# Attention with a bias on one core: scores that stay in PSUM from head to head

## The chip, the cores and the metric

One core of a Trainium2 chip runs the kernel. The metric is the device time of one execution in microseconds (us). Five engines work side by side, each through its own queue in order: TensorE (PE) for matrix products, with its weight loads shown apart (PEld), VectorE (DVE), ScalarE (ACT), GpSimd (POOL), and SyncE (SP), which here only issues transfers (DMAs). Matrix products land in PSUM, a memory of 8 banks, each 128 partitions x 512 float32; everything else lies in SBUF.

## What is computed

```python
batch, n_heads, seq_len, head_dim = 4, 8, 1024, 64          # bias: (1, 1, seq_len, seq_len)
scale = 1.0 / np.sqrt(head_dim)
scores = scale * np.matmul(q, k.transpose(0, 1, 3, 2))
scores = scores + bias
scores_max = np.max(scores, axis=-1, keepdims=True)
attn = np.exp(scores - scores_max) / (np.sum(np.exp(scores - scores_max), axis=-1, keepdims=True) + 1e-8)
return np.matmul(attn, v).astype(np.float32)
```

There are 32 heads of 1024 queries and 1024 keys, all with one bias. Neither kernel subtracts the maximum: the scores are small, and the exps are summed by a column of ones beside v.

## The kernel before

Heads go in 16 pairs (`pr`), queries in halves (`qh`, 512 queries), keys in chunks of 128 (`kc`). A "bank" is one (pair, head, half, chunk): 128 keys x 512 queries of transposed scores, one PSUM bank; there are 512. Three banks share one of two PSUM buffers `ps` (6 of the 8 banks); the last two banks, `xa` and `xb`, serve transposes, the sums `po`, and single banks `pd`.

Per pair, `load_qk` (L75) and `load_v` (L82) issue three kinds of loads on POOL's queue, which cast float32 to bf16 on the way. `transpose_pe` (L86) turns q and k so that the head dimension lies on the partitions: 16 small transposes on PE, then one DVE copy. For q the copy multiplies by `mask`, so that `qT` holds each head beside zeros for the other (L102); `kT` holds both heads of the pair one above the other. `s_fill` (L165) computes three banks with one matmul each, over 128 rows of which the zeros blank out the other head. `s_exp` (L178) is one ScalarE instruction over 128x1536.

The bias enters in two ways. For key chunks of most banks exp(bias) is made once (`b_fill`, `b_exp`, L220 to L233: transposes of `btraw`, then four exps into `eb`), and DVE multiplies each exp by it (`mul_pair`, L235: 1024 or 2048 elements at a time). For the last two chunks of the second half (`late_bias`) PE adds the raw bias, times 1/scale, into PSUM by a second matmul (L176). Six banks, two in each of pairs 3, 7 and 11, have their exp computed on DVE: `d_fill` (L189), `fixed` (L201) and the six steps of `d_steps` (L205), a split into whole and broken powers of two and a polynomial.

`av_bank` (L261) multiplies the exps by v: four pairs of weight load and 65-column matmul a bank, 16 banks to a unit of 512 queries. Its `evac` divides by the ones column on DVE (L279, L281) and SP stores the result. The last pair's second half is done by `av_last` (L296), in two parts.

The order on each engine is written out by a planner (L413 to L764) under `manual_schedule`: it keeps a clock per engine with costs it assumes, and at each turn lets the engine that can start first emit its next piece. The instructions then run in exactly that order, each waiting by semaphores for its inputs. ACT's order is the order of the banks; PE's picks are a fill (`pe_fill`), a transpose (`pe_piece`), a bank for DVE (`pe_d`) or a bank of P times V (`pe_av`).

The lines before that, L327 to L406, start the first pair: part of its k and q comes as float32 on SP's and ACT's queues and is cast on the engines, the first exps are of one and of two banks.

Of the kernel before, what the change touches and what calls it, by code (L numbers as in the profile page):

```python
# [8 lines left out]
F32 = mybir.dt.float32  # L9
# [7 lines left out]
def kernel(  # L17
# [13 lines left out]


    nc = tc.nc
# [6 lines left out]
    HQ = S // 2  # L40
    QC = NCH // 2
# [4 lines left out]
    of = out.rearrange("b h (p c) d -> (b h) p c d", p=P)  # L46
    bf_ = bias.rearrange("a b (p c) k -> p (a b c) k", p=P)

    consts = ctx.enter_context(tc.tile_pool(name="consts", bufs=1))
    raw = ctx.enter_context(tc.tile_pool(name="raw", bufs=3))  # L50
    kvp = ctx.enter_context(tc.tile_pool(name="kvp", bufs=3))
    ep = ctx.enter_context(tc.tile_pool(name="ep", bufs=6))
    op = ctx.enter_context(tc.tile_pool(name="op", bufs=2))
    dp = ctx.enter_context(tc.tile_pool(name="dp", bufs=1))
    de = ctx.enter_context(tc.tile_pool(name="de", bufs=2))
    small = ctx.enter_context(tc.tile_pool(name="small", bufs=4))
    ps_s = ctx.enter_context(tc.tile_pool(name="ps_s", bufs=2, space=bass.MemoryType.PSUM))
    ps_x = ctx.enter_context(tc.tile_pool(name="ps_x", bufs=1, space=bass.MemoryType.PSUM))

    ident = consts.tile([P, P], BF)  # L60
    warm = consts.tile([P, 1], F32)
    btraw = consts.tile([P, NCH, S], BF)
    eb = consts.tile([P, 2, NCH, HQ], BF)
    braw = consts.tile([P, 2, HQ], BF)
    mask = consts.tile([P, 2, HQ], BF)
    vall = consts.tile([P, 2 * NP, NCH, D1], BF)

    k0f = consts.tile([P, 2, QC, D], F32)
    q0f = [consts.tile([P, QC, D], F32, name=f"q0f{t}") for t in range(2)]
    zeros = consts.tile([P, P], BF)  # L70

    raws = {}
    trs = {}

    def load_qk(pr):  # L75
        qr = raw.tile([P, 2, NCH, D], BF, name="qr")
        kr = raw.tile([P, 2, NCH, D], BF, name="kr")
        nc.gpsimd.dma_start(out=kr.rearrange("p t c d -> p t (c d)"), in_=kf[pr])  # L78
        nc.gpsimd.dma_start(out=qr.rearrange("p t c d -> p t (c d)"), in_=qf[pr])  # L79
        raws[pr] = (qr, kr)  # L80
# [5 lines left out]
    def transpose_pe(pr, which, c0, n, tag):  # L86

        src = raws[pr][which]
        px = ps_x.tile([P, n, P], BF, tag=tag, name="px")
        for c in range(n):  # L90
            for t in range(2):
                nc.tensor.transpose(px[t * D:(t + 1) * D, c, :], src[:, t, c0 + c, :], ident[:])  # L92
        if (pr, which) not in trs:
            trs[(pr, which)] = (kvp.tile([P, NCH, P], BF, name="kT") if which else
                                kvp.tile([P, 2, NCH * P], BF, name="qT"))
        dst = trs[(pr, which)]

        def copy():
            if which == 0:

                m = n // QC
                nc.vector.tensor_tensor(  # L102
                    dst[:, :, c0 * P:(c0 + n) * P].rearrange("p t (m q) -> p t m q", m=m),
                    px.rearrange("p (m c) q -> p m (c q)", m=m).unsqueeze(1).to_broadcast([P, 2, m, HQ]),
                    mask.unsqueeze(2).to_broadcast([P, 2, m, HQ]), op=ALU.mult)
            else:
                nc.vector.tensor_copy(dst[:, c0:c0 + n, :], px[:])  # L107
        return copy


    NE = NCH - 2
    DPR = (3, 7, 11)
    banks = [(0, h, 0, kc) for kc in range(NCH) for h in range(2)]

    def mix(early, late, singles):
        while early or late:
            if late and (singles(len(banks), len(early) + len(late)) or not early):
                banks.append(late.pop(0))
            else:
                banks.extend(early[:2])  # L120
                del early[:2]

    for pr in range(NP):
        early = [(pr, h, 1, kc) for kc in range(NE) for h in range(2)]
        late = [(pr, h, 1, kc) for kc in range(NE, NCH - (pr in DPR)) for h in range(2)]
        if pr == NP - 1:
            early = [(pr, h, 1, kc) for h in range(2) for kc in range(NE)]
            late = [(pr, h, 1, kc) for h in range(2) for kc in range(NE, NCH)]
        if pr == 0:
            early += [(1, h, 0, kc) for kc in range(NCH) for h in range(2)]  # L130
            mix(early, late, lambda b, left: b % 3 == 2 and b > 36)
        else:
            if pr > 1:
                banks += [(pr, h, 0, kc) for kc in range(NCH) for h in range(2)]
            mix(early, late, lambda b, left: b % 3 == 2 and (pr < NP - 1 or left > 8))
    NB = len(banks)

    dgroups = []
    for pr in DPR:
        dgroups.append((pr, [len(banks), len(banks) + 1]))  # L140
        banks += [(pr, h, 1, NCH - 1) for h in range(2)]
    assert sorted(banks) == sorted((pr, h, qh, kc) for pr in range(NP) for h in range(2) for qh in range(2) for kc in range(NCH))
    late_bias = {b: x[3] - NE for b, x in enumerate(banks) if x[2] == 1 and x[3] >= NE}
    first_of = {pr: min(b for b in range(NB) if banks[b][0] == pr) for pr in range(NP)}
    d_of = {b: (i, h) for i, (pr, bs) in enumerate(dgroups) for h, b in enumerate(bs)}
    units = {}
    for b in range(len(banks)):
        units.setdefault(banks[b][:3], []).append(b)
    slots = [[0], [1, 2]] + [list(range(i, min(i + 3, NB))) for i in range(3, NB, 3)]
    NS = len(slots)  # L150
    ET = 12
    etiles = {}

    dtiles = {}

    def e_at(b, n):
        if b >= NB:
            return dtiles[d_of[b][0]]["e"][:, d_of[b][1]:d_of[b][1] + n, :]
        if b // ET not in etiles:
            etiles[b // ET] = ep.tile([P, ET, HQ], BF, name="E")  # L160
        return etiles[b // ET][:, b % ET:b % ET + n, :]

    open_ps = {}

    def s_fill(g):  # L165
        if ("S", g) not in open_ps:
            open_ps[("S", g)] = ps_s.tile([P, 3, HQ], F32, tag="s", name="ps")
        ps = open_ps[("S", g)]
        for j, b in enumerate(slots[g]):
            pr, h, qh, kc = banks[b]  # L170
            qT, kT = trs[(pr, 0)], trs[(pr, 1)]
            nc.tensor.matmul(ps[:, j, :], kT[:, kc, :], qT[:, h, qh * HQ:(qh + 1) * HQ],  # L172
                             start=True, stop=b not in late_bias)
        for j, b in enumerate(slots[g]):
            if b in late_bias:
                nc.tensor.matmul(ps[:, j, :], ident[:], braw[:, late_bias[b], :], start=False, stop=True)  # L176

    def s_exp(g):  # L178
        n = len(slots[g])
        nc.scalar.activation(e_at(slots[g][0], n), open_ps.pop(("S", g))[:, :n, :], ACTF.Exp, scale=scale)  # L180

# [5 lines left out]
    LOG2E = 1.4426950408889634  # L187

    def d_fill(b, tag):  # L189
        pr, h, qh, kc = banks[b]  # L190
        ps = ps_x.tile([P, HQ], F32, tag=tag, name="pd")
        nc.tensor.matmul(ps[:], trs[(pr, 1)][:, kc, :], trs[(pr, 0)][:, h, qh * HQ:(qh + 1) * HQ], start=True, stop=False)  # L192
        nc.tensor.matmul(ps[:], ident[:], braw[:, late_bias[b], :], start=False, stop=True)  # L193
        d = d_of[b][0]
        if d not in dtiles:
            dtiles[d] = {"y": dp.tile([P, 2, HQ], I32, name="dy"), "f": dp.tile([P, 2, HQ], F32, name="df"),
                         "p": dp.tile([P, 2, HQ], I16, name="dpw"),
                         "b": dp.tile([P, 2, HQ], F32, name="db"), "e": de.tile([P, 2, HQ], BF, name="de")}

        def fixed():  # L200
            nc.vector.tensor_scalar(dtiles[d]["y"][:, d_of[b][1], :], ps[:], scale * LOG2E * 65536.0, 127.0 * 65536.0,  # L201
                                    op0=ALU.mult, op1=ALU.add)
        return fixed

    def d_steps(d):  # L205
        t = {x: y.rearrange("p h q -> p (h q)") for x, y in dtiles[d].items()}
        t["a"] = t["y"].bitcast(F32)
        lo = t["y"].bitcast(U16).rearrange("p (q w) -> p q w", w=2)[:, :, 0]
        hi = t["y"].bitcast(I16).rearrange("p (q w) -> p q w", w=2)[:, :, 1]
        v = nc.vector  # L210
        return [
            (600, lambda: v.tensor_scalar(t["f"], lo, G / 65536.0, None, op0=ALU.mult)),
            (600, lambda: v.tensor_scalar(t["p"], hi, 0.0, 128.0, op0=ALU.max, op1=ALU.mult)),
            (1140, lambda: v.scalar_tensor_tensor(t["a"], t["f"], U1, t["f"], op0=ALU.add, op1=ALU.mult)),
# [580 lines left out]
```

## Time and profile before

| what | us |
|---|---|
| median of 3 runs (246.30 to 246.69) | 246.63 |
| span of the profiled execution | 246.5 |
| PE idle before fills that waited for an exp (L172, ten times) | 3.3 |
| ACT idle before its first large exp, waiting for PE | 2.6 |
| POOL, loads of v (L84): busy, 32 issues | 28.7 |
| POOL, loads of k and q (L78, L79): busy, 30 issues | 21.2 |
| DVE, products with exp(bias), 2048 elements (L242): busy, 60 | 72.4 |
| DVE, products with exp(bias), 1024 elements (L245): busy, 98 | 64.0 |
| DVE, scaling of results (L281): busy, 63 | 26.7 |
| first exp begins (one bank) / first large exp begins | 5.46 / 9.71 |
| granted PE clock, mean, as a share of full speed | 0.993 |

The profile is of one execution. A row of a group names line, engine, operation, output and inputs, shapes and count; then its busy time in us and the mean duration of one instruction in ns; then the idle time of the engine just before such instructions, and what ended it. Instructions of one engine overlap at their ends, so that the busy time of many is less than count times duration. In the timeline a row has its start, its length, the engine and line, and how many instructions it merges. In the chain of waits the rows have start, length and what the end of the span waited for then.

### The profile page before, as it was taken

Reading aid. Unit: us, or ns where it says so; the run is one execution under the profiler, and the core shown is the slowest. Engines: PE = TensorE matmul, PEld = TensorE weight load, DVE = VectorE, ACT = ScalarE, POOL = GpSimd, SP = SyncE. Lnnn points to the kernel's source line nnn. Section 1 sums busy time; section 2 is a strip of 40 time slices with the busy share of each in tenths; the row PEclk is TensorE's granted clock in tenths of the full one; section 3 lists DMA queues with packets and bytes.
Section 4 is the critical chain, followed back from the end, with each engine's and each line's share of the span. In section 5 each row is a group of like instructions: output and inputs, shape, how many; then the busy total and the mean of one; then the engine's idle time right before and its main releaser. Section 6 shows DMA issues by size and latency. Waiting matters only on the chain.

```text
span 246.5 us, 7234 instructions
## 1 busy us (share of the span) xinstructions
PE 229.9 (93%) x3154; PEld 144.8 (59%) x3207; DVE 219.2 (89%) x366; ACT 236.7 (96%) x181; POOL 55.3 (22%) x76
## 2 busy tenths in 40 slices
PE   8667999999999999999988999999998999999993
PEld 3244656665566656666654665666664566766653
DVE  2417799998999999999999999999999999999994
ACT  5599999999999999999999999999999999999993
POOL 7654333501441304140134000601500000000000
PEclk9799999999999999999999999999999999999999
DMA  5999995995689479492394920792911020202022
GB/s 113 179 197 193 192 131 102 148 84 122 65 123 160 51 122 121 107 116 80 56 127 91 82 88 25 114 122 75 140 45 45 1 88 4 86 1 88 35 77 65
DMA packets 48752, 23.80 MB, mean 97 GB/s; under 512 B 34512, under 2 KB 44624, under 8 KB 48720
## 3 DMA queue, kind: packets, MB, share of 16 engines
q0 software_dynamic: 42560, 14.42, 53.6%
q1 hardware_dynamic: 5872, 8.72, 9.8%
q8 instruction: 25, 0.41, 0.7%
q10 hardware_dynamic: 288, 0.20, 0.3%
q14 instruction: 7, 0.06, 0.1%
HBM read 29.36 MB, written 8.39 MB: 153 GB/s over the span
## 4 chain that ended last, share of the span: by engine, by line
ACT 45%; PE 44%; DVE 4%; DMA 2%; issue 2%; POOL 1%; ACTq 0%; POOLq 0%
ACT E L180 42%; PE ps L172 24%; PE po L269 13%; PE px L92 3%; PE ps L176 3%; ACT eb L232 3%; DMA kr<-in_k_dram 2%; DVE qT L102 1%; DVE E L242 1%; DVE E L239 1%; PE pd L192 1%; PE pd L193 1%; DVE oall L281 1%; DVE db L215 0%; DVE dy L201 0%
## 5 line engine op out<-in xcount | busy, mean ns | idle before, releaser
L180 ACT ACTIVATE E<-ps 128x1536 bf16<-128x1536 f32 (+1 forms) x170 | 227.9, 1525 | 2.8 <-PE ps L172 2.7
L172 PE MATMUL ps<-qT,kT 128*128 128x512 bf16 x454 | 134.9, 382 | 8.2 <-ACT E L180 3.3
L269 PEld LDWEIGHTS <-E 128*128 128x128 bf16 x1992 | 78.9, 98 | 34.1 <-DVE E L242 2.5
L269 PE MATMUL po<-vall,E 128*128 128x65 bf16 x1992 | 84.8, 194 | 0.8 <-DVE E L245 0.3
L242 DVE TENSOR_TENSOR E<-E,eb 128x2048 bf16<-128x2048 bf16 x60 | 72.4, 1217 | 0.0
L245 DVE TENSOR_TENSOR E<-E,eb 128x1024 bf16<-128x1024 bf16 x98 | 64.0, 683 | 4.2 <-ACT eb L232 4.0
L172 PEld LDWEIGHTS <-kT 128*128 128x128 bf16 x506 | 44.9, 97 | 36.6 <-issue 10.2
L84 POOL DMA_DIRECT2D vall<-in_v_dram x32 | 28.7, 902 | 7.1 <-DMA btraw<-in_bias_dram 3.5
L281 DVE TENSOR_TENSOR oall<-po,rs 128x256 f32<-128x256 f32 x63 | 26.7, 425 | 2.2
L78 POOL DMA_DIRECT2D kr<-in_k_dram x15 | 10.5, 699 | 64.5 <-PE px L92 62.4
L102 DVE TENSOR_TENSOR qT<-px,mask 128x2048 bf16<-128x2048 bf16 (+1 forms) x17 | 19.2, 1127 | 5.6 <-PE px L92 5.4
L79 POOL DMA_DIRECT2D qr<-in_q_dram x15 | 10.7, 716 | 48.2 <-PE px L92 47.2
L176 PE MATMUL ps<-braw,ident 128*128 128x512 bf16 x57 | 21.4, 378 | 0.1
L279 DVE RECIPROCAL rs<-po 128x4 f32<-128x4 f32 x63 | 11.2, 178 | 3.3 <-PE po L269 2.5
L107 DVE COPY kT<-px 128x1024 bf16<-128x1024 bf16 (+1 forms) x16 | 10.4, 652 | 0.8 <-PE px L92 0.8
L92 PEld LDWEIGHTS <-qr 128*64 128x64 bf16 x248 | 7.5, 109 | 5.4 <-issue 5.1
L92 PEld LDWEIGHTS <-kr 128*64 128x64 bf16 x240 | 7.2, 109 | 5.0 <-issue 4.7
L92 PE MATMUL px<-ident,qr 128*64 128x128 bf16 x248 | 10.2, 222 | 0.0
L92 PE MATMUL px<-ident,kr 128*64 128x128 bf16 x240 | 9.7, 222 | 0.0
L176 PEld LDWEIGHTS <-ident 128*128 128x128 bf16 x58 | 5.6, 97 | 6.9
L232 ACT ACTIVATE eb<-pb 128x2048 bf16<-128x2048 bf16 (+1 forms) x4 | 6.7, 1676 | 0.0
L226 PEld LDWEIGHTS <-btraw 128*128 128x128 bf16 x56 | 4.0, 146 | 2.0 <-issue 1.6
(59 smaller groups left out, 65.7 us busy)
## 6 DMA issues: line engine op xcount, KB each, us to landing
out_dram<-oall SPq DMA_DIRECT2D x28, 256.0 KB, 2.0
vall<-in_v_dram POOLq DMA_DIRECT2D x32, 128.0 KB, 5.5
kr<-in_k_dram POOLq DMA_DIRECT2D x15, 256.0 KB, 4.3
qr<-in_q_dram POOLq DMA_DIRECT2D x15, 256.0 KB, 4.7
btraw<-in_bias_dram POOLq DMA_DIRECT2D x4, 512.0 KB, 8.7
out_dram<-oall SPq DMA_DIRECT2D x7, 128.0 KB, 1.8
k0f<-in_k_dram SPq DMA_DIRECT2D x2, 128.0 KB, 3.0
q0f<-in_q_dram ACTq DMA_DIRECT2D x1, 128.0 KB, 2.6
```

The lines of the kernel that those rows point to most:

```text
L84: nc.gpsimd.dma_start(out=vall[:, 2 * pr + t, :, :D], in_=vf[pr, :, t])
L92: nc.tensor.transpose(px[t * D:(t + 1) * D, c, :], src[:, t, c0 + c, :], ident[:])
L102: nc.vector.tensor_tensor(dst[:, :, c0 * P:(c0 + n) * P].rearrange("p t (m q) -> p t m q", m=m), px.rearrange("p (m c) q -> p m (c q)", m= ...
L172: nc.tensor.matmul(ps[:, j, :], kT[:, kc, :], qT[:, h, qh * HQ:(qh + 1) * HQ], start=True, stop=b not in late_bias)
L176: nc.tensor.matmul(ps[:, j, :], ident[:], braw[:, late_bias[b], :], start=False, stop=True)
L180: nc.scalar.activation(e_at(slots[g][0], n), open_ps.pop(("S", g))[:, :n, :], ACTF.Exp, scale=scale)
L232: nc.scalar.activation(eb[:, qh, :n, c0 * P:(c0 + 2) * P], open_ps.pop(("B", qh, c0))[:, :n].rearrange("p k c q -> p k (c q)"), ACTF.Exp)
L242: nc.vector.tensor_tensor(e, e, eb[:, qh, kc:kc + 2, :].unsqueeze(2).to_broadcast([P, 2, 2, HQ]), op=ALU.mult)
L245: nc.vector.tensor_tensor(e, e, eb[:, qh, kc:kc + 1, :].to_broadcast([P, n, HQ]), op=ALU.mult)
L269: nc.tensor.matmul(acc[:, i, :], e[:, 0, i * P:(i + 1) * P], vall[:, 2 * pr + h, kc, :], start=(first and i == 0), stop=last, skip_group_c ...
L279: nc.vector.reciprocal(rs[:], acc[:, :, D:D1])
L281: nc.vector.tensor_tensor(oall[:, c0:c0 + QC, :], acc[:, :, :D], rs[:].to_broadcast([P, QC, D]), op=ALU.mult)
```

## The change

The kernel is rewritten around another way of adding the bias. Six PSUM banks become three fixed "places" of 128 keys x 1024, that is, for one chunk of 128 queries all eight key chunks. A place first gets the bias of its query chunk (eight matmuls against `ident8`, the identity times 1/scale). Then a head's scores are added on top and the exp is taken. The next head's fill adds its own scores and removes those of the head before in the same matmul, whose 128 rows hold both heads: k of the one above k of the other, and q with a minus sign for the one to be removed. So the bias is loaded once for each run of heads, and no product with exp(bias) remains.

The unit of work is a slot (place, chunk `c`, head `h`, `start`): 256 slots, one fill of eight 128-column matmuls, one exp of 128x1024 and one P times V of eight 65-column matmuls each. The heads go in three groups of 4, 6 and 6 pairs; in a group all heads pass through chunks 0 to 2, then 3 to 5, then 6 and 7, where the third place takes chunks 6 and 7 of the last third of the group's heads. Two rounds make a batch of up to six slots, whose results share one PSUM bank and one evacuation.

For odd heads the operands are `ko`, `qo`: both heads of the pair, q of the first negated (by `sgn` in the copy out of PSUM). For even heads `ke`, `qe` hold the pair's first head and the pair before's second: `ke` is copied within SBUF by SP's DMAs, `qe` is made on POOL by multiplying with -1. `qs` and the first `qe` of a group have zeros below, for the starts.

Loads of q and k come as float32 on SP's queue into `rawf` (two buffers) and are cast on POOL (k of pair 1 and parts of pair 0 on DVE); v and the bias still come by POOL's casting loads. The exps on DVE are now 18 slots, spread evenly over the full batches, each a chain of seven steps over 1024 elements. The results of a slot are stored by chunk, from SP. The planner is rewritten for the new pieces; P times V runs in the order of the slots, and nine buffers hold exps.

The diff, cut to its core:

```diff
-    ps_s = ctx.enter_context(tc.tile_pool(name="ps_s", bufs=2, space=bass.MemoryType.PSUM))
+    rawf = ctx.enter_context(tc.tile_pool(name="rawf", bufs=2))
+    ps_s = ctx.enter_context(tc.tile_pool(name="ps_s", bufs=1, space=bass.MemoryType.PSUM))
+    places = [ps_s.tile([P, 2, 512], F32, name=f"pl{x}") for x in range(3)]
...
+    ND = 18
+    dslots = [batches[can[(2 * i + 1) * len(can) // (2 * ND)]][5] for i in range(ND)]
...
     def load_qk(pr):
-        qr = raw.tile([P, 2, NCH, D], BF, name="qr")
-        kr = raw.tile([P, 2, NCH, D], BF, name="kr")
-        nc.gpsimd.dma_start(out=kr.rearrange("p t c d -> p t (c d)"), in_=kf[pr])
-        nc.gpsimd.dma_start(out=qr.rearrange("p t c d -> p t (c d)"), in_=qf[pr])
+        f = [rawf.tile([P, 2, NCH, D], F32, name=x) for x in ("q32", "k32")]
+        nc.sync.dma_start(out=f[1].rearrange("p t c d -> p t (c d)"), in_=kf[pr])
+        nc.sync.dma_start(out=f[0].rearrange("p t c d -> p t (c d)"), in_=qf[pr])
+        rawfs[pr] = f
+
+    def cast_qk(pr, both=True):
+        raws[pr] = [raw.tile([P, NCH, 2, D], BF, name=x) for x in ("qr", "kr")]
+        if not both:
+            nc.vector.tensor_copy(raws[pr][1].rearrange("p c t d -> p t c d"), rawfs[pr][1][:])
+        for x in (1, 0) if both else (0,):
+            nc.gpsimd.tensor_scalar(raws[pr][x].rearrange("p c t d -> p t c d"), rawfs[pr][x][:], 1.0, 1.0,
+                                    op0=ALU.mult, op1=ALU.mult)
...
+            if which:
+                nc.vector.tensor_copy(t["ko"][:, cs, :], px[:])
+                if pr not in first_pair:
+                    nc.sync.dma_start(out=t["ke"][:D, cs, :], in_=t["ko"][:D, cs, :])
+                if nxt:
+                    nc.sync.dma_start(out=nxt["ke"][D:, cs, :], in_=t["ko"][D:, cs, :])
             else:
-                nc.vector.tensor_copy(dst[:, c0:c0 + n, :], px[:])
+                nc.vector.tensor_scalar(t["qo"][:, cs, :], px[:], sgn[:], None, op0=ALU.mult)
+                nc.gpsimd.tensor_scalar(t["qe"][:D, cs, :], t["qo"][:D, cs, :], -1.0, 1.0, op0=ALU.mult, op1=ALU.mult)
+                if nxt:
+                    nc.gpsimd.tensor_scalar(nxt["qe"][D:, cs, :], t["qo"][D:, cs, :], -1.0, 1.0, op0=ALU.mult, op1=ALU.mult)
+                if pr in split_pair:
+                    nc.gpsimd.tensor_scalar(t["qs"][:D, cs, :], t["qo"][:D, cs, :], -1.0, 1.0, op0=ALU.mult, op1=ALU.mult)
...
+    def fill(s):
+        x, c, h, start = slots[s]
+        ps = places[x]
+        if start:
+            for kc in range(NCH):
+                nc.tensor.matmul(ps[:, kc // 4, kc % 4 * P:(kc % 4 + 1) * P],
+                                 braw[:, c, :].rearrange("p (kp kc) -> p kc kp", kc=NCH)[:, kc, :], ident8[:],
+                                 start=kc % 4 == 0, stop=False, skip_group_check=True)
+        kk, qq = operands(s)
+        for kc in range(NCH):
+            nc.tensor.matmul(ps[:, kc // 4, kc % 4 * P:(kc % 4 + 1) * P], kk[:, kc, :], qq[:, c, :],
+                             start=False, stop=True, skip_group_check=True)
...
+    def exp(s):
+        etile[s] = ep.tile([P, NCH, P], BF, name="E")
+        nc.scalar.activation(etile[s].rearrange("p c q -> p (c q)"), places[slots[s][0]].rearrange("p b x -> p (b x)"),
+                             ACTF.Exp, scale=scale)
...
+        for kc in range(NCH):
+            nc.tensor.matmul(po[:, j, :], etile[s][:, kc, :], vall[:, h, kc, :], start=j == 0 and kc == 0,
+                             stop=kc == NCH - 1, skip_group_check=True)
```

The start asks for both heads' k of pair 0, three chunks of its q and the first bias rows as float32 on SP's and ACT's queues before anything else:

```diff
+        nc.sync.dma_start(out=k32[:, 0].rearrange("p c d -> p (c d)"), in_=kf[0][:, 0])
+        nc.scalar.dma_start(out=q32[:, :, :C0].rearrange("p t c d -> p t (c d)"), in_=qf[0][:, :, :C0 * D])
+        nc.sync.dma_start(out=b0f[:], in_=bf_[:, 0, :])
+        nc.scalar.dma_start(out=k32[:, 1].rearrange("p c d -> p (c d)"), in_=kf[0][:, 1])
```

## The prediction

> **What bounds the kernel now.** The first view is the page's busy time by engine. The prediction is made against this execution's own span, 246.5 us, which is 0.1 us from the median of the runs (246.63); I treat the two as one scale.
>
> ```profile
> span 246.5 us, 7234 instructions
> PE 229.9 (93%) x3154; PEld 144.8 (59%) x3207; DVE 219.2 (89%) x366; ACT 236.7 (96%) x181; POOL 55.3 (22%) x76
> ACT 45%; PE 44%; DVE 4%; DMA 2%; issue 2%; POOL 1%; ACTq 0%; POOLq 0%
> ```
>
> ScalarE (ACT) leaves 246.5 - 236.7 = 9.8 us unused in the whole span. The chain of waits names PE almost as often as ACT, so the groups by line, with shapes kept apart, come second.
>
> ```profile
> L180 ACT ACTIVATE E<-ps 128x1536 bf16<-128x1536 f32 x167 | 225.4, 1536 | 2.6 <-PE ps L172 2.6
> L232 ACT ACTIVATE eb<-pb 128x2048 bf16<-128x2048 bf16 x2 | 3.8, 1890 | 0.0
> L180 ACT ACTIVATE E<-ps 128x1024 bf16<-128x1024 f32 x2 | 2.1, 1061 | 0.1
> L172 PEld LDWEIGHTS <-kT 128*128 128x128 bf16 x506 | 44.9, 97 | 36.6 <-issue 10.2 <-DVE qT L370 0.3
> L342 POOL MEMSET qT<- 64x512 bf16 x1 | 0.5, 518 | 0.1
> masks.py:199 POOL TENSOR_SCALAR_AFFINE_SELECT ident<-ident 128x128 bf16<-128x128 bf16 x1 | 0.3, 287 | 0.1
> ```
>
> The 167 large exps stand back to back: 2.6 us idle before all of them, at one place in the start. PE is in the chain only because each fill of a PSUM buffer is released by an exp and releases the next. So ACT's own instructions set the time, and PE must merely be early. What PE really needs is read from the chain in order of time, near the end:
>
> ```profile
> 236.84 0.81 PE ps L172 x3
> 237.65 0.61 PE po L269 x20
> ```
>
> Three 512-column matmuls end after 0.81 us, one lasts 382 ns, so they follow each other by (0.81 - 0.38)/2 = 0.215 us, 0.42 ns a column. Twenty pairs of a 128x128 weight load and a 65-column matmul take 0.61 us, 30.5 ns a pair: 27.3 for the columns and 3.2 that the load costs beyond its cover. The timeline of VectorE (DVE) gives starts rather than durations:
>
> ```profile
> 67.08 1.22 DVE L214 SCALAR_TENSOR_TENSOR dy<-df 128x1024 f32<-128x1024 f32 x1
> 68.21 0.68 DVE L107 COPY kT<-px 128x1024 bf16<-128x1024 bf16 x1
> 68.81 0.68 DVE L245 TENSOR_TENSOR E<-E,eb 128x1024 bf16<-128x1024 bf16 x1
> 69.60 0.18 DVE L279 RECIPROCAL rs<-po 128x4 f32<-128x4 f32 x1
> 69.81 0.42 DVE L281 TENSOR_TENSOR oall<-po,rs 128x256 f32<-128x256 f32 x1
> 70.16 1.22 DVE L215 SCALAR_TENSOR_TENSOR db<-df 128x1024 f32<-128x1024 f32 x1
> ```
>
> The 1.22 us form takes 1.13 from start to start, the 0.68 form 0.60, the reciprocal 0.21, the 256-element scaling 0.35.
>
> **ScalarE, the term that decides.** The four exps of the bias go (6.7 us), and the scores' exps become 256 slots of 128x1024, less 18 on DVE: 238. Busy time per instruction is 225.4/167 = 1.350 us at 1536 and 1.77 at 2048 (the chain's time for one), a slope of 0.82 to 0.83 ns an element, so 1024 costs about 0.916. From below, one 1024 lasts 475 ns less than one 1536: 1.350 - 0.475 = 0.875. From above, an exp that no longer overlaps its neighbour costs its whole 1.061. I take 0.916, the line through two rows: 238 x 0.916 = 218.0 us (208.3 at 0.875, 252.5 at 1.061). Before it was 225.4 + 2.1 + 0.6 + 6.7 = 234.8, so 16.8 us leave the bounding engine.
>
> **TensorE.** A score fill is eight pairs of load and 128-column matmul: 128 x 0.42 + 3.2 = 57 ns, 2048 of them 116.7 us. P times V: 2048 x 30.5 = 62.5. Bias starts: ten a group, 30 x 8 transposing matmuls on a strided load; before, 15 such loads took 0.99 us, 66 ns each, so 15.8. Transposes 32 x 8 x 57 = 14.6. Sum 209.6, with a start of about 7 and a tail of 4 about 220: under ACT by some 13 us, at 209.6/218 = 96% of its pace. The place freed by an exp must be refilled (0.46 us) before ACT has done the two other places (1.83 us). I give 2 us of ACT waits for this closeness. The Trainium skill ("TensorE: Matmul & The Clock Gate", section Back-to-back issue gap) states 81 ns sustained for load and matmul pairs at 128 columns; an estimate from it puts the scores at 166 us and PE at 259. The trace's 30.5 ns pair, with the same load under half the columns, speaks against it.
>
> **VectorE.** The multiplications by exp(bias) go (L242, L245, L239: 140 us). The exps on DVE grow from 6 half-size banks to 18 slots: 5 x 1.13 + 2 x 0.60 = 6.85 each, 123 us (the first step reads 1024 from PSUM, 0.60 at 512 plus 0.53). There are 43 evacuations of up to six units: 0.21 + (0.35 + 128/0.96 ns = 0.48) = 0.69, 30 us; single units 18 x 0.15 = 3; copies of q and k 32 x 0.60 = 19; start 4. Sum 179, 40 under today's 219: off the path, hidden by ACT with about 55 us to spare.
>
> **GpSimd (POOL).** It loses 30 casting DMA issues (21 us) and gains 30 casts of 128x1024, 33 negated copies of 64 partitions and 6 memsets. No row shows such a cast. Nearest below: the memset, 518 ns for 512, 1.04 us at 1024. Nearest above: the select, 287 less a fixed 104 (the one-column memset) over 128 elements, 1.43 ns each, 1.57 us. Then 69 operations cost 72 to 108 us, and with V and bias issues (28.7 + 4) 105 to 141 of 236. I take 1.2, nearer the memset because it streams a like row. On average there is room; off the path, if DVE does not pay for it (rival below). Later pairs are transposed up to 60 slots ahead (55 us).
>
> **Queues.** SP takes 30 f32 loads, 26 copies within SBUF (k halves, 64 partitions) and some 124 output stores at about 0.4 us of issue, 72 us. A load of pair x+2 waits for POOL's cast of pair x, and behind it on SP stand stores and k copies. Three output buffers (15 us of batches) and the 60 slots cover 5 us of waiting; without that cover each of 12 loads would cost a few us.
>
> **Start and tail.** The first fill now needs bias rows, both heads' k whole and three chunks of q: 1.2 MB at once. The page's SP queue moved 8.72 MB in 9.8% of the span, 361 GB/s: 3.3 us, plus 0.75 to issue and 2 to land, 6.0. Then cast (0.4), eight cold transposes (1.0), copy (0.7), eight cold matmuls (0.9): first exp at 9.0, when before ACT had already done 1.7 us of exps and the large ones began at 9.71. Pairs 1 to 3 are then wanted at slots 6, 12 and 18 (25.5 us). POOL has about nine operations, 9 issues and the pair's two casts ahead of pair 3's transposes: 6.5 + 11 + 7 + 2.4 = 27, then transposes, copy, SBUF copy 3. I charge 3 us (0 to 9) to the start. The tail from last exp to end was 4.8; one unit's P times V, one evacuation and a store make 4.5.
>
> **Sum.** 9.0 + 218.0 + 2 + 3 + 4.5 = 236.5 us. The bounds of ACT's price and the start alone give 224 to 243.
>
> **Rivals.**
>
> TensorE takes over. At 66 ns, the strided row, scores cost 135 and PE 228; with start, tail and the waits of two engines at one pace, about 242. For it: 96%. Against: contiguous weights. At 77 ns, half of the 97 ns load uncovered, scores cost 158, PE 251, the time 262. The Trainium skill's 81 ns would be this case.
>
> The start is short of data: POOL's operations at 1.57 and 6 MB of loads in 27 us hold slots back by 9 instead of 3: 243.
>
> GpSimd holds DVE up, and the kernel gets slower. The mechanism: POOL's 63 reading operations and DVE's steps on SBUF operands exclude each other, so a DVE step waits for whatever POOL has begun, and the evacuations queue behind it. Place: the 18 chains. It decides once the waits pass the 55 us of spare, 0.9 us for each of the 63. At a full 1.2 us each, DVE needs 179 + 76 = 255, and with the start 262. For it: 72 two-input steps (81 us) and 36 others meet 76 us of POOL. Against: the two meet only part of the time; at a half it is 38 us, within the spare. No trace here has a POOL operation that reads beside a busy DVE. The Trainium skill ("SBUF — State Buffer", section Who interferes with whom) states such a lock, for VectorE instructions with two SBUF inputs or in a two-port mode, the second comer blocked for the whole instruction.
>
> The change doesn't do what it says: the subtraction works in PSUM but each slot waits for its fill, exps cost 1.061, and the time is 252.5 + 18 = 270.
>
> **Chances.** Forecast 0.58 (own range 230 to 241). TensorE at 66 ns 0.12, at 77 ns 0.04. Late start 0.09. GpSimd against DVE 0.13. No overlap 0.04. What a measurement here can tell from no change is 0.2%, 0.5 us. Faster: the forecast 0.57, the late start 0.07, the 242 case 0.09 = 0.73. Slower: 0.13 + 0.04 + 0.04, and 0.04 from the upper edges of the others = 0.25. Within 0.2%: 0.02. The range 228 to 252 reaches over the 242 and 243 cases and a third of GpSimd's, where the waits pass the spare only a little; it leaves out the 262 and 270 cases and a corner below 228 (ACT near 0.88), 0.19 in all.
>
> **What would show it.** Right: exps of 128x1024 with 0.90 to 0.92 us busy each and idle time before them under 6 us after the start; PE's fill of eight near 0.46 us; DVE under 200 us. Wrong: POOL casts or DVE steps far above 1.2 us and ACT waiting for fills that waited for DVE or for P times V; fills of 0.6 us; a first exp after 11 us, or a gap near 25 us longer than 5.

## The result, and the profile after

The changed kernel takes 291.6 us (median of 4 runs, 290.1 to 292.8) where the kernel before takes 246.5 beside it: 1.183 times as long, 95% interval 1.179 to 1.188. One execution of run 12 below (279.1) fell in a slower state of the chip and is left out of its time. The prediction was 236.5, range 228 to 252. Its profiled execution has a span of 288.8 us. The page's engine rows, the clock and DMA rows of its forty slices (7.2 us each), and the shares of the chain of waits:

```profile
span 288.8 us, 10500 instructions
PE 235.1 (81%) x4598; PEld 226.5 (78%) x4598; DVE 201.5 (70%) x275; ACT 225.1 (78%) x241; POOL 120.1 (42%) x114
PEclk9977599699999999795999999999979999999997
DMA  7999909992087399989421499317281111010211
PE 34%; DMA 19%; DVE 18%; ACT 9%; issue 8%; POOL 7%; SPq 2%; ACTq 1%; DVEq 0%; POOLq 0%
```

ScalarE is busy 225.1 us, 11.6 less than before, so the work did go down. But no engine is busy over 81%, and ACT's 45% of the chain fell to 9%: it now waits for others, among them transfers, VectorE and GpSimd. The groups by line, shapes kept apart:

```profile
L205 ACT ACTIVATE E<-pl 128x1024 bf16<-128x1024 f32 x238 | 222.6, 1065 | 53.8 <-PE pl L198 51.2 <-PE po L264 2.4
L198 PE MATMUL pl<-qe,ke 128*128 128x128 bf16 x784 | 63.6, 231 | 25.8 <-DMA ke<-ko 23.5 <-DVE dy L225 0.8 <-ACT E L205 0.6
L244 DVE SCALAR_TENSOR_TENSOR db<-db,dpw 128x1024 f32<-128x1024 f32 x18 | 25.1, 1393 | 0.4
L230 DVE TENSOR_SCALAR df<-dy 128x1024 f32<-128x1024 uint16 x18 | 17.0, 946 | 0.5
L234 DVE TENSOR_SCALAR dpw<-dy 128x1024 int16<-128x1024 int16 x18 | 16.8, 934 | 0.0
L135 POOL TENSOR_SCALAR qr<-q 128x1024 bf16<-128x1024 f32 x15 | 20.8, 1388 | 9.6 <-DMA q<-in_q_dram 9.6
```

The exps stood idle for 53.8 us (2.87 of it before the first), nearly all for fills; the fills of even heads in turn waited 23.5 us for `ke`, the k copied within SBUF. Two of the same steps of VectorE before the change:

```profile
L216 DVE SCALAR_TENSOR_TENSOR db<-db,dpw 128x1024 f32<-128x1024 f32 x3 | 3.6, 1215 | 0.0
L212 DVE TENSOR_SCALAR df<-dy 128x1024 f32<-128x1024 uint16 x3 | 2.1, 685 | 0.0
```

The step with 1215 ns before is at 1393, that with 685 at 946, and its neighbour (683 before) at 934. ScalarE's timeline (start, length, instructions merged, idle time before) shows where the waits lie:

```profile
10.08 1.02 ACT L205 ACTIVATE E<-pl 128x1024 bf16<-128x1024 f32 x1 [2.87 <-PE pl L198]
11.78 4.70 ACT L205 ACTIVATE E<-pl 128x1024 bf16<-128x1024 f32 x5 [0.68 <-PE pl L198]
33.48 11.25 ACT L205 ACTIVATE E<-pl 128x1024 bf16<-128x1024 f32 x12 [17.00 <-PE pl L198]
53.51 4.69 ACT L205 ACTIVATE E<-pl 128x1024 bf16<-128x1024 f32 x5 [8.78 <-PE pl L198]
58.54 3.80 ACT L205 ACTIVATE E<-pl 128x1024 bf16<-128x1024 f32 x4 [0.34 <-PE pl L198]
```

Six exps run (one head pair in three places), then 17 us of nothing, twelve, then 8.8 us of nothing. The span adds up as 10.1 (first exp) + 222.8 (exps) + 26.8 (waits up to 62 us) + 23.9 (waits after that, in dozens of pieces, the longest 5.3) + 5.2 (tail) = 288.8. Against the forecast's terms that is +1.1, +4.8, +45.7 (waits of 50.7 for 2 + 3) and +0.7. The 46 us of waits are what has to be explained, in two halves.

**The early half.** From the chain in order of time (start, length, what was waited for):

```profile
2.12 10.06 DMA q<-in_q_dram
...
12.36 1.05 POOL qr L135
...
13.43 4.28 DMA q<-in_q_dram
...
18.76 0.92 POOL vall L140
...
21.89 0.37 SPq L126
...
22.31 10.05 DMA ke<-ko
...
32.41 2.74 PE pl L198 x24
...
36.27 0.26 PE po L264 x8
36.53 0.45 PE pl L198 x8
...
44.06 8.28 DMA ke<-ko
```

Pair 1's q takes 10 us to land among the other loads; the cast follows, and SP, in order, holds the `ke` copy of pair 1 back behind loads of later pairs that wait for casts on a GpSimd busy with issuing loads of v. Issued at 22.31, the copy itself lands 10 us later: the DMA row shows 9 tenths in most slices up to 36 us. When the fills come, the granted clock of that slice is 0.5, and 24 matmuls take 2.74 us, 114 ns each; from 36 us on eight take 0.45, 56 ns each. At 44 us the next copy takes 8.28 us to land. SP's own waits over the whole span (what, total us, times, longest):

```profile
SPq L125 <- POOL kr L135: 55.1, 11, 14.9
SPq L126 <- DMA q<-in_q_dram: 5.4, 2, 3.4
SPq L126 <- POOL qr L337: 2.1, 1, 2.1
```

The last two rows fall before the copy at 22.31, with 2.3 us of waits for `qr` of L135: 9.8 us by then. Of the 55.1 for `kr` casts none does; 20.6 come before 62 us.

**The late half.** The timelines of VectorE and of GpSimd side by side, around 126 us, where the stretch is greatest:

```profile
125.73 3.26 DVE L230 TENSOR_SCALAR df<-dy 128x1024 f32<-128x1024 uint16 x1
128.91 1.52 DVE L234 TENSOR_SCALAR dpw<-dy 128x1024 int16<-128x1024 int16 x1
130.47 1.22 DVE L237 SCALAR_TENSOR_TENSOR dy<-df 128x1024 f32<-128x1024 f32 x1
```

```profile
126.38 1.06 POOL L173 TENSOR_SCALAR qe<-qo 64x1024 bf16<-64x1024 bf16 x1
127.39 1.05 POOL L135 TENSOR_SCALAR kr<-k 128x1024 bf16<-128x1024 f32 x1
128.40 1.49 POOL L135 TENSOR_SCALAR qr<-q 128x1024 bf16<-128x1024 f32 x1
```

A step of 0.69 us lasts 3.26 and ends 0.55 us after the second GpSimd operation; the next GpSimd operation then lasts 1.49 instead of 1.04, and the next step 1.52. After that GpSimd has none of these until the next pair, and the step at 130.47 takes its 1.22. Over all 18 chains the six steps after the first last 0.92 us more than alone, 16.6 us in all, and GpSimd's casts and negations 16.7 us more than at 1.04. What that costs in time the trace can't say; the runs must.

### The profile page after: what moved, and what is told of

The parts are those of the page before. It is cut to its first block, busy times and chain, and to the rows that moved or that the text cites. A ratio compares the mean times of both kernels' runs of the same rounds, so it can differ in the third digit from the quotient of the medians.

```text
span 288.8 us, 10500 instructions
## 1 busy us (share of the span) xinstructions
PE 235.1 (81%) x4598; PEld 226.5 (78%) x4598; DVE 201.5 (70%) x275; ACT 225.1 (78%) x241; POOL 120.1 (42%) x114
## 4 chain that ended last, share of the span: by engine, by line
PE 34%; DMA 19%; DVE 18%; ACT 9%; issue 8%; POOL 7%; SPq 2%; ACTq 1%; DVEq 0%; POOLq 0%
PE pl L198 20%; DMA ke<-ko 10%; PE po L264 10%; ACT E L205 9%; DMA q<-in_q_dram 5%; DVE dy L225 3%; PE pl L193 3%; POOL qr L135 2%; POOL kr L135 2%; DMA out_dram<-ob 2%; DVE de L248 2%; DVE df L230 2%; DVE db L244 2%; DMA out_dram<-od 2%; DVE db L237 2%
## 5 line engine op out<-in xcount | busy, mean ns | idle before, releaser
L205 ACT ACTIVATE E<-pl 128x1024 bf16<-128x1024 f32 x238 | 222.6, 1065 | 53.8 <-PE pl L198 51.2
L198 PE MATMUL pl<-qe,ke 128*128 128x128 bf16 x784 | 63.6, 231 | 25.8 <-DMA ke<-ko 23.5
L198 PEld LDWEIGHTS <-ko 128*128 128x128 bf16 x1264 | 77.2, 99 | 3.2 <-DVE ko L166 0.2
L198 PE MATMUL pl<-qo,ko 128*128 128x128 bf16 x1024 | 76.5, 220 | 0.9
L198 PEld LDWEIGHTS <-ke 128*128 128x128 bf16 x784 | 51.6, 104 | 28.8 <-DMA ke<-ko 24.8
L173 POOL TENSOR_SCALAR qe<-qo 64x1024 bf16<-64x1024 bf16 (+1 forms) x16 | 21.4, 1336 | 88.3 <-DVE qo L172 75.8
L140 POOL DMA_DIRECT2D vall<-in_v_dram x32 | 30.5, 952 | 0.0
L244 DVE SCALAR_TENSOR_TENSOR db<-db,dpw 128x1024 f32<-128x1024 f32 x18 | 25.1, 1393 | 0.4
L135 POOL TENSOR_SCALAR qr<-q 128x1024 bf16<-128x1024 f32 x15 | 20.8, 1388 | 9.6 <-DMA q<-in_q_dram 9.6
L248 DVE SCALAR_TENSOR_TENSOR de<-dy,db 128x1024 bf16<-128x1024 f32 x18 | 23.9, 1331 | 0.3
L275 DVE TENSOR_TENSOR ob<-po,rs 128x384 f32<-128x384 f32 (+2 forms) x43 | 22.6, 527 | 1.5
L237 DVE SCALAR_TENSOR_TENSOR dy<-df 128x1024 f32<-128x1024 f32 x18 | 22.9, 1274 | 0.5
L237 DVE SCALAR_TENSOR_TENSOR db<-df 128x1024 f32<-128x1024 f32 x18 | 23.2, 1286 | 0.0
L193 PE MATMUL pl<-ident,braw 128*128 128x128 bf16 x240 | 20.6, 231 | 2.3 <-DVE dy L225 2.0
L135 POOL TENSOR_SCALAR kr<-k 128x1024 bf16<-128x1024 f32 x14 | 18.0, 1288 | 0.8
```

The source lines that it names most:

```text
L135: nc.gpsimd.tensor_scalar(raws[pr][x].rearrange("p c t d -> p t c d"), rawfs[pr][x][:], 1.0, 1.0, op0=ALU.mult, op1=ALU.mult)
L140: nc.gpsimd.dma_start(out=vall[:, 2 * pr + t, :, :D], in_=vf[pr, :, t])
L193: nc.tensor.matmul(ps[:, kc // 4, kc % 4 * P:(kc % 4 + 1) * P], braw[:, c, :].rearrange("p (kp kc) -> p kc kp", kc=NCH)[:, kc, :], ident8[ ...
L198: nc.tensor.matmul(ps[:, kc // 4, kc % 4 * P:(kc % 4 + 1) * P], kk[:, kc, :], qq[:, c, :], start=False, stop=True, skip_group_check=True)
L205: nc.scalar.activation(etile[s].rearrange("p c q -> p (c q)"), places[slots[s][0]].rearrange("p b x -> p (b x)"), ACTF.Exp, scale=scale)
L237: w.scalar_tensor_tensor(o[:], t["f"][:], c, t["f"][:], op0=ALU.add, op1=ALU.mult)
```

## The experiments

Every kernel here computes the whole function. In runs 3 to 9 the planner, given other slots or costs, may also write another order; in 1 and 2, and in 10 to 12 beside 8, the order of the pieces stays. Waits of ScalarE are read from its timeline as in the sum above, "early" up to 62 us and "late" after; times are medians, beside 246.2 to 246.5 for the kernel before.

| run | edit to the kernel after | us | ratio to before, 95% interval | first exp | early | late |
|---|---|---|---|---|---|---|
| after | | 291.6 | 1.179 to 1.188 | 10.1 | 26.8 | 23.9 |
| 1 | `ke` copied by VectorE | 282.1 | 1.139 to 1.148 | 10.3 | 13.6 | 27.6 |
| 2 | loads of q, k from GpSimd's queue | 284.6 | 1.148 to 1.160 | 10.0 | 22.5 | 22.1 |
| 3 | no exps on VectorE | 280.4 | 1.129 to 1.145 | 11.1 | 25.8 | 1.0 |
| 4 | q, k cast by their loads | 263.1 | 1.060 to 1.077 | 10.3 | 12.9 | 8.9 |
| 5 | 4, all copies and 17 slots on VectorE | 274.0 | 1.111 to 1.121 | 10.3 | 4.8 | 27.3 |
| 6 | 5 with 9 slots on VectorE | 255.9 | 1.036 to 1.043 | 10.7 | 7.0 | 2.3 |
| 7 | 1 and 3 together | 272.5 | 1.104 to 1.110 | 10.1 | 13.8 | 3.4 |
| 8 | 4, start reordered, early copies on VectorE | 254.1 | 1.030 to 1.033 | 9.3 | 5.6 | 9.1 |
| 9 | 8 with 14 slots on VectorE | 253.0 | 1.025 to 1.029 | 10.0 | 5.2 | 4.9 |
| 10 | 8 and 26 idle casts on GpSimd | 266.8 | 1.081 to 1.088 | 9.6 | 5.1 | 21.4 |
| 11 | 8 and 26 idle memsets on GpSimd | 260.9 | 1.051 to 1.061 | 9.2 | 5.6 | 15.7 |
| 12 | 8 and 26 idle copies on VectorE | 277.1 | 1.113 to 1.128 | 9.3 | 10.8 | 26.1 |

**Run 1: is it the copies of k?**

```diff
-                    nc.sync.dma_start(out=t["ke"][:D, cs, :], in_=t["ko"][:D, cs, :])
+                    nc.vector.tensor_copy(t["ke"][:D, cs, :], px[:D])
...
-                    nc.sync.dma_start(out=nxt["ke"][D:, cs, :], in_=t["ko"][D:, cs, :])
+                    nc.vector.tensor_copy(nxt["ke"][D:, cs, :], px[D:])
```

> The 26 copies of k halves into ke go from DMAs on SP's queue to copies by VectorE straight out of PSUM; the order of everything else stays. Theory (the ke copies come late, because they stand on SP's queue behind loads that wait for casts, and then share the DMA engines with those loads): the gaps of ScalarE of 17.0, 8.8 and 5.3 us close almost wholly, and the time falls from 291 to 250 to 262 us, with 26 x 0.6 = 16 us more of VectorE. Rival (GpSimd's casts and negated copies are late themselves, so the pairs' operands are late in any case): 280 or more, with ScalarE waiting at the same slots. Rival (VectorE is the bound): 291 or more, since it gets 16 us more work.

282.1: far less gained than I expected. The early waits halve, so the copies were the last link there, but only the last. Of the wait of 17.0 us 8.7 stay. The chain, and below it GpSimd's timeline, show what is late next, the v and GpSimd's negated q:

```profile
13.59 7.06 DMA vall<-in_v_dram
...
20.79 2.81 PE po L264 x48
...
23.83 1.06 POOL qe L173
```

```profile
22.04 1.77 POOL L140 DMA_DIRECT2D vall<-in_v_dram  x2
```

TensorE, in order, waits with pair 0's P times V for v until 20.65, and `qe` of pair 1 starts on GpSimd only at 23.83. GpSimd's own queue held it about as long: two issues of v stand ahead of it and end at 23.80. Late, nothing is gained: VectorE carries 26 copies more.

**Run 2: is it SP's order?** The loads of q and k are issued from GpSimd's queue (`nc.gpsimd.dma_start` in `load_qk`), so that nothing on SP waits for casts.

> The 30 loads of q and k (float32, uncast) are issued on GpSimd's queue, so that nothing that waits for a cast stands before the ke copies on SP's queue; the bytes moved are the same. If the wait in SP's queue is the larger part of the lateness: the first ke copy is issued some 8 us earlier than at 22.3 us, and the time falls to 262 to 275 us. If sharing the DMA engines with the bulk of the loads is the larger part: the copies still take 6 to 10 us to land and the time stays within 283 to 295. If GpSimd's lateness is the cause: slower than 291, as GpSimd gets 30 issues of 0.7 us more.

284.6, and the first wait is still 17.3 us. The first `ke` copy of pair 1 did go out 8 us earlier, and it landed within 2.2 us; but now the fill waits for `qe`, which GpSimd reaches at 30.89 instead of 24.70, behind loads that it issues (rows of SP, GpSimd and TensorE):

```profile
14.05 0.46 SPq L168 DMA_DIRECT2D ke<-ko  x1
...
30.89 1.09 POOL L173 TENSOR_SCALAR qe<-qo 64x1024 bf16<-64x1024 bf16 x1
...
32.03 2.72 PE L198 MATMUL pl<-qe,ke 128*128 128x128 bf16 x24 [6.30 <-POOL qe L173]
```

So the time fell into the range of one branch (copies that land late) with that branch's sign absent, and the run puts no price on SP's order: its edit made another operand as late. The second wait halves (8.8 to 4.2).

**Run 3: no exps on VectorE** (`ND = 0`; ScalarE does all 256).

> No exp on VectorE (ND = 0): ScalarE gets 18 more exps, 18 x 0.93 = 17 us, and VectorE loses its chains, so that GpSimd's operations meet almost no two-input step of VectorE. Theory of the late ke copies: the gaps at the start stay, and the time rises to 298 to 308 us. Rival (VectorE's chains and GpSimd hold each other up and make the operands late): casts and negated copies all take 1.04 us instead of up to 2.0, the small gaps after 60 us go, and the time is 280 to 290.

280.4: faster than the kernel after with 18 exps more on ScalarE. The late waits vanish (1.0), the early ones stay (25.8). GpSimd's timeline, with the same casts and negations, now shows

```profile
70.49 1.04 POOL L135 TENSOR_SCALAR kr<-k 128x1024 bf16<-128x1024 f32 x1
71.50 1.04 POOL L135 TENSOR_SCALAR qr<-q 128x1024 bf16<-128x1024 f32 x1
```

1.04 us for each, none over 1.06. So the halves are separate, and the late one needs VectorE's chains.

**Run 7: runs 1 and 3 together.**

> The copies of ke by VectorE (as e1) and no exp on VectorE (as e3) together. If the start and the chains are two separate causes, the gains add: 291.6 - 9.5 - 11.2 = 271 us, with one gap of about 9 us at slot 6 left and then ScalarE without gaps. If both removed the same waits: 279 to 282.

272.5. The gains of 9.5 and 11.2 us make 20.7, measured 19.1: they add, as for two causes.

**Runs 4 to 6: GpSimd's work taken away.** In run 4 the loads of q and k cast, as in the kernel before; TensorE pays with sixteen half-width transposes instead of eight.

```diff
+        raws[pr] = [raw.tile([P, 2, NCH, D], BF, name=x) for x in ("qr", "kr")]
+        for x, src in ((1, kf), (0, qf)):
+            nc.gpsimd.dma_start(out=raws[pr][x].rearrange("p t c d -> p t (c d)"), in_=src[pr])
```

> q and k of pairs 1 to 15 are cast by the loads on GpSimd's queue, as before the change; 29 casts of 1.04 us and more leave GpSimd, and no load stands on SP's queue. ke is still copied by SP's DMAs, and the negated copies stay on GpSimd. Theory (two causes: at the start the operands of pairs 1 to 3 come late through GpSimd's and SP's queues and full DMA engines; later GpSimd's operations and VectorE's chains block each other): about half of both goes, 262 to 276 us, VectorE's four two-input steps a mean under 1.30 us each. Rival (the gaps come from VectorE's load alone, whatever GpSimd does): 283 or more.

263.1: 28 us gained, 14 early and 15 late. With GpSimd's casts go the loads that waited on SP's queue, and the cast q and k have five buffers instead of three, so the gain isn't that of the casts alone. Run 5 also gives `ke`, `qe` and `qs` to VectorE, from PSUM, with 17 slots; run 6 is the same with 9.

> As e4, and GpSimd computes nothing after the start: ke, qe and qs are written by VectorE straight from PSUM (33 + 26 more copies of 0.6 us, 35 us), 17 exps on VectorE instead of 18, three buffers for their results instead of two, the loads of v ahead of those of q and k that are needed later, and the order of work written out with these costs. Theory of the two causes: VectorE's steps all take 1.22 and 0.68 us, ScalarE runs without gaps over 1 us after the start, first gap under 6 us: 240 to 254 us. Rival (VectorE's load alone): it now has 35 us more work, so 283 or more.

> As e5 with 9 exps on VectorE instead of 17: ScalarE gets 8 x 0.92 = 7.4 us more, VectorE 55 us less. If VectorE's queue still holds back copies in e5, this one is faster than e5; if e5 is bound by ScalarE alone, it is 7 us slower.

Run 5 is a miss, 274.0. VectorE's steps are back at 1.22 and 0.69 to 0.72 in the mean, next to no exclusion is left, and yet ScalarE's timeline has

```profile
84.34 10.19 ACT L201 ACTIVATE E<-pl 128x1024 bf16<-128x1024 f32 x11 [3.02 <-PE po L260]
103.60 1.94 ACT L201 ACTIVATE E<-pl 128x1024 bf16<-128x1024 f32 x2 [9.07 <-PE po L260]
```

VectorE's own timeline has a chain from 88.2 to 94.3, evacuations, and then eleven copies of 0.67 to 0.75 us one after the other, 96.9 to 104.1. TensorE waits in order behind transposes whose PSUM those copies empty; its P times V stands behind them, and ScalarE, whose exp buffers are full, waits for that (po). (The last of these transposes starts at 101.78, when a load of q lands; the copies had freed its PSUM 0.15 us earlier, so the load hardly adds to it.) With 9 slots (run 6) the late waits are 2.3 and the time 255.9, though ScalarE has eight exps more. So a full VectorE queue is enough by itself.

**Runs 8 and 9: the start.** Run 8 is run 4 with the start repaired: copies for pairs 0 to 3 on VectorE, loads of v and of the next pairs issued from GpSimd before its compute, and thirteen wide matmuls on zeros while TensorE waits.

```diff
         load_v(0)
-        cast_qk(2)
+        load_qk(2)
         load_v(1)
         nc.gpsimd.dma_start(out=braw[:, 3, :], in_=bf_[:, 3, :])
+        load_qk(3)
         nc.gpsimd.tensor_scalar(qr0[:, C0:].rearrange("p c t d -> p t c d"), q32[:, :, C0:], 1.0, 1.0,
                                 op0=ALU.mult, op1=ALU.mult)
         for c in (4, 5):
             nc.gpsimd.dma_start(out=braw[:, c, :], in_=bf_[:, c, :])
-        load_qk(3)
```

> e4 (casts by the loads) with a reordered start: for pairs 0 to 3 ke, qe and qs are written by VectorE from PSUM, POOL issues the loads of v and of the next pairs without computing in between, 13 wide matmuls on zeros keep TensorE at work until the first data, three buffers for the results of VectorE's exps. From pair 4 on SP's copies and GpSimd's negated copies stay. If the first gap of e4 (9.3 us) is the late operands of pair 1, it shrinks under 3 us and the time falls by 6 to 10 us, to 252 to 257; if something else holds slot 6 back, the gap and 260 or more stay. First exp 1 us earlier if the zeros warm TensorE's clock.

254.1, as expected. ScalarE's timeline begins

```profile
9.28 5.80 ACT L215 ACTIVATE E<-pl 128x1024 bf16<-128x1024 f32 x6 [1.99 <-PE pl L208]
16.84 7.44 ACT L215 ACTIVATE E<-pl 128x1024 bf16<-128x1024 f32 x8 [1.77 <-PE pl L208]
```

and the wait of 17.0 is 1.77. From after to run 8 the early waits fall by 21.2 and the late ones by 14.8. Run 9, with 14 slots, gains another microsecond:

> e8 with 14 exps on VectorE: 4 x 0.92 = 3.7 us more for ScalarE. If VectorE's queue still costs gaps, equal to e8 or faster (247 to 254); if not, 3 to 4 us slower than e8.

253.0: four exps more cost ScalarE 3.0 us busy, and 4.2 us of late waits go. It is the best version found, still 2.7% slower than before.

**Runs 10 to 12: the disputed costs put back one at a time** into run 8, each 26 operations whose results nobody reads, at the same places:

```diff
     def cast_qk(pr, both=True):
-        pass
+        for x in range(2): nc.gpsimd.tensor_scalar(b0f[:], q32.rearrange("p t c d -> p (t c d)"), 1.0, 1.0, op0=ALU.mult, op1=ALU.mult)
```

The edit is against run 8, where this function does nothing. Run 11 has `nc.gpsimd.memset(b0f[:], 0.0)` there, run 12 `nc.vector.tensor_copy(b0f[:], ...)`.

> e8 plus 26 casts of 128x1024 on GpSimd into a tile that nothing reads, at the places where the changed kernel has its casts. Nothing waits for their results. Theory (GpSimd's operations and VectorE's steps on SBUF hold each other up): VectorE's two-input steps and the two short steps get slower again, up to 2.0 us where they meet a cast, and the time rises by 4 to 12 us against e8. Rival (no such blocking, what cost time was only waiting for the casts' results): within 2 us of e8.

> The kernel with the repaired start (254.1 us, 26 casts of q and k done by the loads), and at the 26 places where the idle GpSimd casts stood (266.8 us), 26 memsets of 128x1024 float32 that nobody waits for. A memset reads nothing; by the 518 ns for 512 elements it takes about 1.0 us, as a cast alone does, so GpSimd's queue is as full, with 26 us more. Theory A (the casts cost because reading GpSimd operations and VectorE's steps hold each other up): the memsets keep about 1.0 us whatever VectorE does, VectorE's two-input steps stay at 1.23 to 1.31, and the time is 254 to 258. Theory B (the casts cost because what stands behind them on GpSimd's own queue, the negated q, the loads, comes late): 262 to 268, with VectorE's steps unchanged all the same. If the memsets too are stretched or stretch VectorE's steps to 1.3 to 1.4, the exclusion isn't one of reading operations and A and B can't be told apart here.

> The same kernel, with 26 copies of 128x1024 float32 on VectorE at those places, which nobody waits for, in place of the idle GpSimd casts: by the 0.69 us of its other copies, or 1.2 us of its slower form, 18 to 31 us more in VectorE's queue, about the 16.6 us by which its steps were stretched in the kernel after, and no more work on GpSimd. Theory C (VectorE's queue is so full that whatever is put into it comes back as ScalarE waits, the exclusion being one way of filling it): 262 to 270. Theory A alone (the stretched GpSimd operations matter as much): 255 to 260.

The groups by line, of runs 10, 11 and 12 in turn:

```profile
L129 POOL TENSOR_SCALAR b0f<-q 128x1024 f32<-128x1024 f32 x26 | 37.0, 1422 | 1.9
L258 DVE SCALAR_TENSOR_TENSOR de<-dy,db 128x1024 bf16<-128x1024 f32 x18 | 24.2, 1346 | 0.3
```

```profile
L132 POOL MEMSET b0f<- 128x1024 f32 x26 | 26.2, 1009 | 1.3
L261 DVE SCALAR_TENSOR_TENSOR de<-dy,db 128x1024 bf16<-128x1024 f32 x18 | 22.0, 1220 | 0.3
```

```profile
L132 DVE COPY b0f<-q 128x1024 f32<-128x1024 f32 x26 | 25.7, 988 | 0.5
```

The casts cost 12.7 us, the memsets 6.7, both almost wholly in the late waits. The memsets keep 1.01 us and stretch VectorE's six steps by 2.7 us in all over run 8; the casts take 1.42 and stretch them by 8.9. The memsets' 260.9 lies between my two expectations (254 to 258, 262 to 268): about half of a cast's cost comes with the place it takes in GpSimd's queue (that it is the negations and loads behind it that come late is inferred), and the other half appears only where the operation reads. Run 12 was beyond both expectations (255 to 260, 262 to 270): 25.7 us put into VectorE's queue come back as 23.0 us of time. Run 8's page, without them, has VectorE idle for 51.6 us:

```profile
span 252.3 us, 10936 instructions
PE 232.7 (92%) x4845; PEld 217.4 (86%) x4845; DVE 200.7 (80%) x289; ACT 224.7 (89%) x241; POOL 96.9 (38%) x106
```

Run 12 isn't pure, since these copies too meet GpSimd's 24 negations, and the early waits grow by 5; but there is no slack of the kind that the forecast assumed.

## Why the prediction was wrong

**The step that failed first** is the paragraph on queues: "Three output buffers (15 us of batches) and the 60 slots cover 5 us of waiting", and so no charge for SP. It did name the right wait (a load waits for the cast two pairs back, and k copies stand behind), but it tested the cover against the steady state and not the start, where pairs 1 to 3 are wanted at slots 6, 12 and 18 and no slots lie in between. SP had waited 9.8 us for q loads and their casts when it issued pair 1's copies, and these landed up to 10.1 us later. The start was charged 3 us, at most 9; the early waits are 26.8. The "SBUF copy 3" took 10 among the loads, and pair 1's q, which got no price of its own, 10.06. The rival that the start is short of data (0.09, at 243) had the right place and a third of the size. And the sum followed GpSimd's queue only to pair 3, not TensorE's order, in which pair 0's P times V waited for v (run 1). Of the first wait, 17.0 us, 8.3 go with the copies of k (run 1); the rest is v and GpSimd's `qe`, behind its issues. Run 8 shows the size: 21 us come back when the loads cast and the start is reordered.

**The second** is that VectorE, at 179 us, is "off the path, hidden by ACT with about 55 us to spare". Of 201.5 busy, 16.6 are the stretch and about 6 are under-counted. But the error isn't in the sum; spare time over the whole span is not slack at the moment when a copy is due. TensorE takes transposes, fills and P times V in one written order, so a copy late by a few us stops the fills, and three places last ScalarE under 3 us. Run 12 shows 0.9 us of time for each us put in, at 51.6 us of apparent spare (252.3 - 200.7 in run 8); run 5 shows it with next to no exclusion.

**The rival GpSimd against DVE** (0.13, at 262) had the right mechanism and the wrong point of decision. It let the waits decide only past the 55 us of spare; they cost time at 16.6 already. The Trainium skill ("SBUF — State Buffer", section Who interferes with whom) states an exclusive lock on a port pair that VectorE and GpSimd share, the second comer blocked. The trace agrees for the steps on SBUF operands (3.26 and 1.52 for 0.69 in the rows above), and in both directions: GpSimd's operations too are stretched, from 1.04 to as much as 2.0. As to how the late half divides: runs 3, 8, 10 and 11 show that most of it needs both VectorE's chains and GpSimd's casts, and that of the casts about half is queue and half exclusion in run 8's setting. What each is worth in the kernel after, where SP's order is a third part, stays open.

**Right, or off by a size.** First exp 10.1 for 9.0. The exp: 0.935 us busy each for 0.916, 0.9225 in undisturbed stretches (24 in 22.14), which makes 1.6 of the 4.8 us; the rest is lost overlap, about 0.1 us (1.02 for a lone exp, less 0.92) at each of some 31 breaks. Nor was 0.916 the line through the prediction's two rows: 1.350 at 1536 and 1.77 at 2048 give 0.93 at 1024, and 221.3 us instead of 218.0. The rival without overlap fell: the mean duration is 1065 ns, and still 222.6/238 is 0.935. Tail 5.2 for 4.5. TensorE was right: a fill of eight 0.45 us, 56 ns a pair for 57; P times V 32 ns a pair for 30.5; the bias about 63 for 66; so neither TensorE rival came. The 81 ns that the Trainium skill ("TensorE: Matmul & The Clock Gate", section Back-to-back issue gap) gives for such pairs at 128 columns isn't seen in the steady part, where a pair takes 56. GpSimd's operation was taken at 1.2: alone 1.04, met 1.29 to 1.39. Its total was about right; "on average there is room" was the wrong question.

Even without any wait, run 8's own terms make 9.3 + 222.4 + 5.9 = 237.6 us of span, 3.6% under the span before. By these terms it is about the most, with that start and tail, that this way of adding the bias could bring with 18 slots on VectorE, and run 9 still has 10 us of waits.

## What to carry to other kernels

Busy sums against the span bound a change only if every engine could take its work in any order; for each operand that is newly made on another engine, follow one copy from load to first use through each queue at the start, where no earlier work covers it, and charge landing times from a stretch as full of loads as that one. An engine with 50 us to spare can still be the limit if a third engine takes its results in a fixed order with two or three buffers; put an idle operation into its queue and see how much of it comes back. Work given to GpSimd beside long VectorE chains on SBUF operands was paid twice here, in its queue and in the stretch (12.7 us for 26 idle casts, 6.7 for as many memsets), so let the loads cast where they can.

## What the runs showed of the hardware

- The same 128 KB copy within SBUF landed 2.2 us after its issue at best, 6.4 in the median and 10.1 at worst, those over 8 us while the DMA row stood at 9 tenths.
- GpSimd's tensor_scalar over 1024 elements takes 1.04 us alone, on 128 partitions from float32 as on 64 from bf16, and up to 2.0 beside VectorE's steps; a memset of 128x1024 float32 keeps 1.01 in the mean beside them.
- VectorE's copies out of PSUM were not stretched: the 8 of `ko` that ran beside a GpSimd operation took 686 ns, the 8 others 685. Its steps on SBUF operands were.
- After the 17 us wait, TensorE's matmuls came at half pace (114 ns for 56) while the granted clock read 0.5.
